# Re-timing the row gathers of a PEER layer: slot transfers, early loads, weight rows and a gate pass moved

## The chip, the cores and the metric

The kernel runs on one core of one Trainium2 chip. The metric is the device time of one execution in microseconds (us); lower is better. The time before is 1664.05 us, the median of three executions (1662.84 to 1665.58).

## What is computed

One decoder layer over 256 tokens of width 2048: two kinds of attention, a layer norm, the PEER block, a second norm, a gated embedding and a third norm. The change touches the PEER block alone. In the reference it is, cut short:

```
q = (xt @ wq).reshape(t, 8, 256)                 # 8 heads, two halves a and b
sa, sb = q_a @ keys[0].T, q_b @ keys[1].T        # 128 scores for each half
va, ia = top_k(sa, 16);  vb, ib = top_k(sb, 16)
top, sel = top_k(va[..., :, None] + vb[..., None, :], 16)
eidx = (ia * 128 + ib)[sel];  gates = softmax(top)
act = gelu(u[eidx] . x);  out = sum(gates * act * v[eidx])
```

So each token picks 16 of 16384 experts in each of 8 heads, and needs the 2048 numbers of each picked expert's row in two tables, `u` and `v` (128 MB each).

## The kernel before, in words

**Two ways through the experts.** For the first 88 tokens (`NSP`) the rows are gathered token by token. One such *sparse gather* (L1042) brings 128 rows, 1 MB, into one of four buffers `gb`, and VectorE multiplies it: 88 gathers of `u` rows (L1008, dot products), then 88 of `v` rows (L1018, weighted sums `y`). That makes 176. For the other 168 tokens (`NDT`) the kernel works densely by blocks of 128 experts. A first part of the experts (`SEG1`, 56 blocks) takes `u` whole: `u_block` multiplies a block of `u` with the tokens and keeps the activations in `A0`, `A1`. For the remaining 72 blocks' worth, only experts that some token picked are listed: 48 *listed* blocks (`NBLK[1]`), gathered into `uf` (L1400), transposed and multiplied. The `v` side has 39 *gathered* blocks for the first part (`NBLK[0]`) and 48 listed ones, each a 1 MB gather into `vf` or `vx` (L1400) and sixteen 128x128 matrix multiplications (L1489, each shown as two records) with 128 or 168 token columns, as `cols` says.

**The order of the stages** is: query and scores head half by head half (16 steps `hh`); dense `u` (56 blocks); listed `u` (48 blocks); `v` of the 39 gathered blocks; `v` of the 48 listed ones; the residuals and the second norm; the gated embedding.

**Weights of the gathered blocks.** After dense `u`, a first gate pass (`all_gates`, `gate_work`) multiplies the gates into `A0`, `A1`; these go to the scratch `s_w` in HBM by eight transfers on SyncE's queue, and each gathered block fetches its 128 weight rows back with a gather of its own into `wc`. A second gate pass does the same for the listed blocks' weights, `WL`. It has 57 groups of up to three tokens (14 for the 40 tokens of the first half, 43 for the 128 of the second), and nearly every group takes two steps of the generator, 118 in all. `half`, called twice in each gathered block, runs them. For each group VectorE makes one-hot tables (L715, L1098), ScalarE scales (L1096), TensorE multiplies into `ps_G` (L1107, L1108), VectorE multiplies into `WL` (L1116).

**What sets the order.** Generators are advanced at fixed places by `run`. The sparse gathers are paced by `gathers(n)`, which adds `n` to a running sum and starts one gather for each whole unit; the constants `GQ`, `GU`, `GUF`, `GUT`, `GUL`, `GV` are gathers per step or block of each stage. The result of gather k is used when gather k+3 is started. A scheduler with a time estimate of its own then fixes each engine's instruction order at build time; from there on every engine takes its instructions in that order. All row gathers (sparse, `uf`, `vf`, `vx`, `wc`) and the small *slot transfers* `eig` (L825), which lay out the picked expert numbers for the sparse gathers, are issued by GpSimd (POOL).

**The top-k of the first 128 tokens** is done by `topk_work` in batches of heads (`BATCH`): first head and count. A batch's top-k on VectorE is followed by `head_slots`, which computes the expert numbers (L821) and issues the slot transfer (L825). Then the generator does the other 128 tokens' top-k (`second`), and beside it `first_flags`, which first transposes the picked indices of the first 128 tokens on TensorE (`index_T`, L856).

**Early loads.** Five blocks of `u` are loaded ahead into `early`, one at each of the steps hh = 2 to 6; the dense `u` stage uses them first.

Of the kernel before, what the change touches and what calls it, by code (L numbers as in the profile page):

```python
# [9 lines left out]
F32 = mybir.dt.float32  # L10
# [9 lines left out]
P = 128  # L20
# [26 lines left out]
NBLK = tuple(map(sum, CAPS))  # L47
# [10 lines left out]
NDT = T - NSP  # L58
# [1 line left out]
SELB = 8  # L60
CAND = ((0, 3, 16), (3, 16, 4))
NCAND = sum((i1 - i0) * w for i0, i1, w in CAND)
BATCH = ((0, 1), (1, 2), (3, 2), (5, 2), (7, 1))
NGB = 4


GQ = 1.7
GU, GUF, GUT = 0.80, 0.92, 0.50
GUL, GV = (1.10, 1.50), (0.62, 0.88)
GSCALE = 2.0 ** 15  # L70
GB = 3

EARLY, HEARLY = 5, 2
OHB = 4

STAG, LEAD, NVX = 3, 4, 4
FBC = 12
NZERO = 3
WF = 5
# [90 lines left out]
def build(tc, a, out):  # L170
    nc = tc.nc
    pools = Pools(tc)
# [20 lines left out]
    at = pools.open("at", "left", bufs=2)  # L193
# [95 lines left out]
    def load(dst, src):  # L289
        tc.keep_in_program_order(nc.sync.dma_start(dst, src))  # L290
# [262 lines left out]
    def ln_rows(pool, which):  # L553
        gr = pool.tile([P, D], F32, name="g_row", tag="g_row")
        br = pool.tile([P, D], F32, name="b_row", tag="b_row")
        load(gr, a["ln_g"][which:which + 1, :].to_broadcast([P, D]))
        load(br, a["ln_b"][which:which + 1, :].to_broadcast([P, D]))
        return gr, br
# [53 lines left out]
    def affine(xt, c, gr, br):  # L612
        s = slice(c * 512, (c + 1) * 512)
        nc.gpsimd.tensor_tensor(xt[:, s], xt[:, s], gr[:, s], op=ALU.mult)
        nc.gpsimd.tensor_tensor(xt[:, s], xt[:, s], br[:, s], op=ALU.add)
# [3 lines left out]
    def spill_x1():  # L619
        gr, br = ln_rows(rowp, 0)  # L620
        yield 4
        for c in range(NCH):
            affine(x1[0], c, gr, br)
            yield 4
        load(a["s_x1"], x1[0])
        spilled.append(0)
# [78 lines left out]
    keep = tc.keep_in_program_order  # L705
# [112 lines left out]
    def head_slots(h):  # L818

        c = slice(h * TOPK, (h + 1) * TOPK)  # L820
        nc.vector.scalar_tensor_tensor(eg[:NSPR, 0, h], iaN[:NSPR, 0, c], float(NKEY),  # L821
                                       ibN[:NSPR, 0, c], op0=ALU.mult, op1=ALU.add)
        t0, n = GROUPS[0]
        m = n // PH
        nc.gpsimd.dma_start(  # L825
            eig[0][:, 0, h * m:(h + 1) * m],
            eg[t0:t0 + n, 0, h].rearrange("t (r c) -> t r c", c=m))

    def topk_work():
        nc.vector.tensor_copy(io128, io128f)  # L830
        for h0, n in BATCH:
            for _ in topk_heads(0, h0, n):
                pass
            for h in range(h0, h0 + n):
                head_slots(h)
            yield
        for i in range(1, len(GROUPS)):
            slots(i, 0, by_slot(i, 0))

        second, first, flags = topk_heads(1, 0, PH), gates(0), first_flags()  # L840
        for step, _ in enumerate(second):
            if step > 2:
                next(first, None)
            next(flags, None)
            yield
        for _ in first:
            pass
        yield from index_T(1)
        yield from second_flags(gates(1), flags)
# [117 lines left out]
    def gathers(n):  # L967

        nonlocal due
        due += n  # L970
        while due >= 1:
            due -= 1
            run(sparse, 1)
# [243 lines left out]
    idxV, idxW, over = {}, {}, []  # L1217
# [117 lines left out]
    def run(work, n):  # L1335

        for _ in range(n):
            if next(work, "end") == "end":
                return True
        return False  # L1340
# [9 lines left out]

    steps = 1
    work = topk_work()
    sparse = sparse_work()
    bg.add(spill_x1(), 4)
    for hh in range(2 * PH):
        if hh == HEARLY:

            assert spilled
            pools.close("rowp", "x1p")
            lsp = pools.open("lsp", "right", bufs=1)  # L1360
            iaT, ibT = (lsp.tile([P, T, 2], F16, name=nm) for nm in ("iaT", "ibT"))
            iaF, ghf = (lsp.tile([P, T], F32, name=nm) for nm in ("iaF", "ghf"))
            gl2 = lsp.tile([P, T, 2], F16, name="gl2")
            a0p = pools.open("a0p", "right", bufs=1)
            A0 = a0p.tile([P, SEG0, NDT], F32, name="A0")
            earlyp = pools.open("earlyp", "right", bufs=1)
            early = [earlyp.tile([P, D], F32, name=f"early{ia}") for ia in range(EARLY)]
        if HEARLY <= hh < HEARLY + EARLY:
            load(early[hh - HEARLY], a["peer_u"][hh - HEARLY])
        query(hh)  # L1370
        if hh in [2 * (h0 + n) for h0, n in BATCH]:
            run(work, 1)
        if hh > 2:
            gathers(GQ)
    bg.flush()
    run(work, 1)
    for ia in range(SEG1):
        if ia == EARLY:
            pools.close("earlyp")
            a1p = pools.open("a1p", "right", bufs=1)  # L1380
# [12 lines left out]
    marked = False  # L1393
    order = [(i, b) for i in range(2) for b in range(NBLK[i])]

    def cols(i, b):
        return (N0, P) if b < CAPS[i][0] else (0, NDT)

    def rows_of(dst, src, idx, b):
        keep(nc.gpsimd.indirect_dma_start(  # L1400
            out=dst, out_offset=None, in_=src,
            in_offset=bass.IndirectOffsetOnAxis(ap=idx[:, b:b + 1], axis=0),
            bounds_check=src.shape[0] - 1, oob_is_err=False))
        return dst

    def WL_of(b):
        c0 = min(b, CAPS[1][0]) * P + max(b - CAPS[1][0], 0) * NDT
        return WL[:, c0:c0 + cols(1, b)[1]]

    def slot(name):  # L1410
        return sup.tile([P, D], F32, name=name, tag="wf", bufs=WF)

    fetched = []
    taken = 0

    def fetch():
        nonlocal taken
        i, b = order.pop(0)
        k = taken % (WF + NVX)
        taken += 1  # L1420
        if k % 2 and k < 2 * NVX and not i and b < NBLK[0] - WF:
            vf = vxp.tile([P, D], F32, name="vx", tag="vx", bufs=NVX)
        else:
            vf = slot("vf")
        if i:
            w = WL_of(b)
        else:
            c0, n = cols(i, b)
            w = wcp.tile([P, NDT], F32, name="wc", tag="wc", bufs=WF + NVX + 1)
            rows_of(w, a["s_w"].rearrange("p a t -> (p a) t"), idxW[i], b)  # L1430
            w = w[:, c0:c0 + n]
        rows_of(vf, a["v_rows"], idxV[i], b)
        fetched.append((i, b, vf, w))

    def rows_T(uf, c, pool, tpool):

# [14 lines left out]
    stored = False  # L1451
    work = all_gates(ohp, A0, A1, WL)
# [13 lines left out]
    for k in range(2):  # L1466
        turn(k)
    for b in range(NBLK[1]):
        if b == NBLK[1] - LEAD:
            assert stored  # L1470
            pools.close("a1p", "a0p")
            vxp = pools.open("vxp", "right", bufs=1)
            wcp = pools.open("wcp", "right", bufs=1)
        ps = pbank(pp, "ps_u")
        c0, n = cols(1, b)
        for c in range(4):
            turn(4 * b + c + 2)
            rows_mm(ps, turned.pop(0), c, c0, n)
            if b >= 2 and (c or n > P) and not stored:
                run(work, 1)  # L1480
        keep(nc.scalar.activation(WL_of(b), ps[:, :n], AF.Gelu_apprx_tanh))
        if b >= NBLK[1] - LEAD:
            fetch()
        gathers(GUL[n > P])
    pools.close("utp")
    def v_mm(d, i, b, vf, w, last):
        c0, n = cols(i, b)
        o = psv[d // 3][:, d % 3 * NDT + c0:d % 3 * NDT + c0 + n]
        return nc.tensor.matmul(o, vf[:, d * P:(d + 1) * P], w, start=False,  # L1489
                                stop=last and (d % 3 == 2 or d == ND - 1))  # L1490
# [16 lines left out]
    def v_blocks(n, ahead, between=lambda d: None):  # L1507

        for _ in range(n):
            while order and len(fetched) <= (ahead if order[0] < (0, NBLK[0] - WF) else LEAD):  # L1510
                fetch()
            block = fetched.pop(0)
            for d in range(ND):
                v_mm(d, *block, False)
                if d % 8 == 7:
                    between(d)
            gathers(GV[cols(*block[:2])[1] > P])

    psv = [v_bank(pp, 3 * NDT) for _ in range(4)] + [v_bank(pa, n * NDT) for n in (3, 1)]
    done = False  # L1520

    def half(d):
        nonlocal done
        if not done:
            done = run(work, 2)

    for b in range(NBLK[0]):
        if b == NBLK[0] - LEAD:
            more = nc.values_load(total[0:1, 0:1], min_val=0, max_val=NIA * NKEY)
        v_blocks(1, LEAD + NVX, half)  # L1530
    assert done
    for dst, src in zip(("s_ia", "s_ib", "s_gl"), (iaT, ibT, gl2)):
# [99 lines left out]
    with tc.If(more > 0, preferred_fallthrough_block=True, label="rest"):  # L1632
# [5 lines left out]
        for ia in range(NIA):  # L1638
            i = int(ia >= SEG1)
            vf, uf, _ = spare  # L1640
            nc.gpsimd.dma_start(vf, a["v_rows"][ia * NKEY:(ia + 1) * NKEY, :])
            wc = fbp.tile([P, NDT], F32, name="wc_", tag="wc_")
# [395 lines left out]
```

## Time and profile before

| | us |
|---|---|
| median of three executions | 1664.05 |
| the profiled execution | 1664.92 |
| its span, first to last instruction | 1663.1 |
| TensorE busy in it | 1610.7 |
| VectorE / ScalarE / GpSimd busy | 1056.0 / 735.7 / 603.1 |
| data moved | 518.53 MB, mean 312 GB/s |

The stages in the span: query from about 414 to 534, dense `u` to 824, listed `u` to 1132, `v` of the gathered blocks to 1300.9, the end of the second gate pass alone to 1318.6, `v` of the listed blocks to 1554. In the profile PE is TensorE, DVE VectorE, ACT ScalarE, POOL GpSimd, SP SyncE. A row of a timeline gives the start, the duration, the engine and line, and in brackets the idle time before it with what ended it; a row of waits gives who waited for whom, then total us, number and longest. The rows themselves stand in the prediction.

### The profile page before, as it was taken

The numbers are of one execution on the slowest core, as the hardware profiler recorded it, in microseconds if no ns is written. First come the engines' busy times: TensorE is split into PE (matmuls) and PEld (weight loads), VectorE is DVE, ScalarE is ACT, GpSimd is POOL, SyncE is SP. The second block draws the span as 40 slices with busy tenths as digits, with TensorE's granted clock in tenths as the row PEclk, the third lists the DMA queues.
The fourth block names the chain that finished last, engine by engine and source line by source line (L and its number), as shares of the span: only waits on it lengthen the run. The fifth ranks groups of instructions, "written<-read, shape, count | busy, mean of one in ns | idle before, by whom it ended". The sixth has DMA issues, their size and how long they took to land. (4 is left out here: it accounts for less than half of the span.)

```text
span 1663.1 us, 30575 instructions
## 1 busy us (share of the span) xinstructions
PE 1610.7 (97%) x11666; PEld 1491.9 (90%) x11666; DVE 1056.0 (63%) x2557; ACT 735.7 (44%) x1740; POOL 603.1 (36%) x538
## 2 busy tenths in 40 slices
PE   9999999999999899999999999999999698899998
PEld 7888888877889899999999999998999688899787
DVE  5555488865377899676667888723455844450776
ACT  5687458753111276956566666530222200000552
POOL 0133023201244425121544434556886755521000
PEclk9999999999999999999999999999999799999999
DMA  8654654475798699999999999999999999996571
GB/s 297 199 164 153 239 166 140 161 301 184 297 377 343 266 422 409 390 359 374 354 421 388 369 346 346 364 344 411 412 380 367 357 421 420 421 386 205 200 269 51
DMA packets 90606, 518.53 MB, mean 312 GB/s; under 512 B 12300, under 2 KB 15436, under 8 KB 38314
## 3 DMA queue, kind: packets, MB, share of 16 engines
q0 software_dynamic: 47984, 330.83, 50.5%
q1 hardware_dynamic: 40742, 182.55, 30.0%
q10 hardware_dynamic: 1728, 3.15, 0.5%
q8 instruction: 92, 1.51, 0.4%
q14 instruction: 60, 0.49, 0.1%
HBM read 508.47 MB, written 10.18 MB: 312 GB/s over the span
## 5 line engine op out<-in xcount | busy, mean ns | idle before, releaser
L131 DVE TENSOR_TENSOR wl<-wf,wh 128x1024 fp32r<-128x1024 f32 (+1 forms) x199 | 212.7, 1091 | 139.3 <-ACT wh L130 137.6
L130 ACT CAST wh<-wf 128x1024 fp32r<-128x1024 f32 (+1 forms) x199 | 172.0, 892 | 258.6 <-DMA wf<-ple_gate 145.9
L1018 DVE SCALAR_TENSOR_TENSOR y<-gb,ew,y 128x2048 f32<-128x2048 f32 x78 | 183.2, 2349 | 145.7 <-DMA gb<-v_rows,eig 144.5
L221 PE MATMUL ps_u<-XF,wf 128*128 128x168 f32 x1632 | 251.3, 311 | 0.0
L221 PEld LDWEIGHTS ps_u<-XF,wf 128*128 128x128 f32 x1632 | 235.5, 191 | 3.0
L1489 PE MATMUL ps_v<-WL,vf 128*128 128x128 f32 (+1 forms) x1536 | 204.9, 297 | 18.0 <-DMA vf<-v_rows,idxV 15.5
L1448 PE MATMUL ps_u<-XF,uT 128*128 128x128 f32 (+1 forms) x1536 | 220.2, 288 | 0.0
L1489 PEld LDWEIGHTS ps_v<-WL,vf 128*128 128x128 f32 x1536 | 201.4, 200 | 20.4 <-DMA vf<-v_rows,idxV 17.2
L1008 DVE SCALAR_TENSOR_TENSOR gb<-gb,xq 128x2048 f32<-128x2048 f32 x88 | 200.5, 2285 | 22.6 <-DMA gb<-u_rows,eig 21.4
L1448 PEld LDWEIGHTS ps_u<-XF,uT 128*128 128x128 f32 x1536 | 199.1, 191 | 0.7
L209 PE MATMUL ps_qk<-X,wh 128*128 128x512 f32 x512 | 185.2, 401 | 0.0
L1042 POOL DMA_INDIRECT gb<-u_rows,eig x88 | 105.3, 1196 | 210.0 <-DVE eqb L715 42.7
L1442 ACT COPY uT<-ps_T 128x512 f32<-128x512 f32 x192 | 111.7, 587 | 115.4 <-PE ps_T L1439 115.0
L1042 POOL DMA_INDIRECT gb<-v_rows,eig x88 | 131.5, 1494 | 53.4 <-issue 20.4
L1096 ACT ACTIVATE hi<-eq,ghf 128x56 f16<-128x56 f16 (+2 forms) x336 | 87.0, 325 | 141.4 <-DVE eq L715 137.8
L211 PE MATMUL ps_qk<-X,wl 128*128 128x256 f32 x512 | 145.7, 285 | 0.0
L1400 POOL DMA_INDIRECT vf<-v_rows,idxV x72 | 92.0, 1278 | 113.0 <-PE ps_v L1489 85.8
L209 PEld LDWEIGHTS ps_qk<-X,wh 128*128 128x128 f32 x512 | 96.4, 188 | 21.9 <-issue 1.0
L1439 PE MATMUL ps_T<-ident,uf 128*128 128x128 f32 x768 | 113.1, 274 | 2.4 <-DMA uf<-u_rows,idxV 2.4
L221 PE MATMUL ps_q<-XF,wf 128*128 128x256 f32 x512 | 114.6, 381 | 0.2 <-ACT eb L590 0.2
L221 PEld LDWEIGHTS ps_q<-XF,wf 128*128 128x128 f32 x512 | 96.1, 191 | 13.2 <-ACT eb L590 0.9
L1400 POOL DMA_INDIRECT uf<-u_rows,idxV x48 | 60.3, 1257 | 123.2 <-PE ps_T L1439 112.6
(366 smaller groups left out, 2909.6 us busy)
## 6 DMA issues: line engine op xcount, KB each, us to landing
wf<-peer_u SPq DMA_DIRECT2D x51, 1024.0 KB
wf<-w_qk SPq DMA_DIRECT2D x64, 512.0 KB
wf<-w_out SPq DMA_DIRECT2D x32, 512.0 KB
wf<-peer_wq SPq DMA_DIRECT2D x16, 1024.0 KB
wf<-ple_gate SPq DMA_DIRECT2D x16, 1024.0 KB
wf<-w_v SPq DMA_DIRECT2D x16, 512.0 KB
wf<-w_sv SPq DMA_DIRECT2D x15, 512.0 KB
early<-peer_u SPq DMA_DIRECT2D x5, 1024.0 KB
```

Source lines behind the costliest of these rows:

```text
L130: self.order(nc.scalar.copy(wh, src))
L131: self.order(nc.vector.tensor_tensor(wl, src, wh.bitcast(F32), op=ALU.subtract))
L209: nc.tensor.matmul(ps, wh[:, j * P:(j + 1) * P], xt[:, dt, :], start=dt == 0, stop=False)
L211: nc.tensor.matmul(ps[:, :T], wl[:, j * P:(j + 1) * P], xt[:, dt, :T], start=False, stop=dt == ND - 1)
L221: nc.tensor.matmul(ps[:, :T - t0], wf[:, dt * P:(dt + 1) * P], xt[:, dt, t0:], start=dt == 0, stop=dt == ND - 1)
L1008: keep(nc.vector.scalar_tensor_tensor(g, g, 1.0, xq[i], op0=ALU.mult, op1=ALU.mult, accum_out=eact[i][:, j:j + 1]))
L1018: keep(nc.vector.scalar_tensor_tensor(ys[i], g, ew[i][:, j:j + 1], ys[i], op0=ALU.mult, op1=ALU.add))
L1042: keep(nc.gpsimd.indirect_dma_start(out=g, out_offset=None, in_=a[kind], in_offset=bass.IndirectOffsetOnAxis(ap=eig[i][:, 0, j:j + 1], axi ...
L1400: keep(nc.gpsimd.indirect_dma_start(out=dst, out_offset=None, in_=src, in_offset=bass.IndirectOffsetOnAxis(ap=idx[:, b:b + 1], axis=0), bo ...
L1439: nc.tensor.transpose(ps[:, j * P:(j + 1) * P], uf[:, (4 * c + j) * P:(4 * c + j + 1) * P], ident)
L1448: nc.tensor.matmul(ps[:, :n], uT[:, j * P:(j + 1) * P], XF[:, d, NSP + c0:NSP + c0 + n], start=d == 0, stop=d == ND - 1)
L1489: return nc.tensor.matmul(o, vf[:, d * P:(d + 1) * P], w, start=False, stop=last and (d % 3 == 2 or d == ND - 1))
```

## The change

Five edits, made together:

1. `BATCH` becomes (0,1), (1,1), (2,2), (4,2), (6,2), and a `yield` stands between a batch's top-k and its slot transfers, so the transfers are issued one step hh later than the top-k (`starts`). The last batch has two heads instead of one, and its slot transfers come in the first dense `u` block. `first_flags` starts at step 6 of `second` instead of step 0.
2. The five early loads are issued at hh = 6, 8, 10, 12, 14.
3. In the last four listed `u` blocks only the four row transfers `vf` are issued, all into slots that `uf` leaves; the pools of `vx` and `wc` are opened after the last listed `u` block, and the weight rows `wc` follow then, ordered behind the last of these transfers (`issue_after(behind.ins)`). The order of slots and extra buffers changes with it: five slots, then four `vx`.
4. `half` runs 4 steps a block only in the first eight gathered blocks and 3 after that, instead of 4 throughout.
5. The rates: `GQ` 1.7 to 2.0; 2.2 gathers a block (`GUE`) in the last six listed `u` blocks, instead of 1.5; `GV` from 0.62 and 0.88 (narrow and wide blocks) to 0.42 and 0.80 for the gathered and 0.42 and 0.85 for the listed blocks.

```
-BATCH = ((0, 1), (1, 2), (3, 2), (5, 2), (7, 1))
+BATCH = ((0, 1), (1, 1), (2, 2), (4, 2), (6, 2))
-GQ = 1.7
+GQ = 2.0
-GUL, GV = (1.10, 1.50), (0.62, 0.88)
+GUL, GUE = (1.10, 1.50), 2.20
+GV = (0.42, 0.80), (0.42, 0.85)
-EARLY, HEARLY = 5, 2
+HEARLY, WHEN = 2, (6, 8, 10, 12, 14)
+EARLY = len(WHEN)
...
             for _ in topk_heads(0, h0, n):
                 pass
+            yield
             for h in range(h0, h0 + n):
                 head_slots(h)
             yield
...
-            next(flags, None)
+            if step > 5:
+                next(flags, None)
...
-        if HEARLY <= hh < HEARLY + EARLY:
-            load(early[hh - HEARLY], a["peer_u"][hh - HEARLY])
+        if hh in WHEN:
+            k = WHEN.index(hh)
+            load(early[k], a["peer_u"][k])
         query(hh)
-        if hh in [2 * (h0 + n) for h0, n in BATCH]:
+        if hh in starts or hh - 1 in starts:
             run(work, 1)
...
-        if k % 2 and k < 2 * NVX and not i and b < NBLK[0] - WF:
+        if k >= WF and not i and b < NBLK[0] - WF:
             vf = vxp.tile([P, D], F32, name="vx", tag="vx", bufs=NVX)
...
+    def weights():
+        for block in fetched:
+            i, b, _, w = block
+            if w is None:
+                c0, n = cols(i, b)
+                w = wcp.tile([P, NDT], F32, name="wc", tag="wc", bufs=WF + NVX + 1)
+                rows_of(w, a["s_w"].rearrange("p a t -> (p a) t"), idxW[i], b)
+                block[3] = w[:, c0:c0 + n]
...
-        gathers(GUL[n > P])
+        gathers(GUL[n > P] if b < NBLK[1] - LEAD - 2 else GUE)
     pools.close("utp")
+    assert stored
+    pools.close("a1p", "a0p")
+    vxp = pools.open("vxp", "right", bufs=1)
+    wcp = pools.open("wcp", "right", bufs=1)
+    with tc.issue_after(behind.ins):
+        weights()
+        for _ in range(NVX + 1):
+            fetch()
+            weights()
...
-            gathers(GV[cols(*block[:2])[1] > P])
+            gathers(GV[block[0]][cols(*block[:2])[1] > P])
...
-            done = run(work, 2)
+            done = run(work, 1 + (d < 8 or at < 8))
```

More of the change, by code (lines that the diff above doesn't have):

```diff
@@ L1354, in build @@
     bg.add(spill_x1(), 4)
+    starts = [2 * (h0 + n) for h0, n in BATCH]
     for hh in range(2 * PH):
@@ L1394, in build @@
     order = [(i, b) for i in range(2) for b in range(NBLK[i])]
+    behind = None
     def cols(i, b):
@@ L1399, in rows_of @@
     def rows_of(dst, src, idx, b):
-        keep(nc.gpsimd.indirect_dma_start(
+        nonlocal behind
+        behind = keep(nc.gpsimd.indirect_dma_start(
             out=dst, out_offset=None, in_=src,
@@ L1424, in fetch @@
             vf = slot("vf")
[L1425 to L1431, printed above, removed]
-        rows_of(vf, a["v_rows"], idxV[i], b)
-        fetched.append((i, b, vf, w))
+        rows_of(vf, a["v_rows"], idxV[i], b)
+        fetched.append([i, b, vf, WL_of(b) if i else None])
+    def weights():
[6 more added lines that the diff above has]
+                block[3] = w[:, c0:c0 + n]
     def rows_T(uf, c, pool, tpool):
@@ L1468, in build @@
     for b in range(NBLK[1]):
[L1469 to L1473, printed above, removed]
         ps = pbank(pp, "ps_u")
@@ L1511, in v_blocks @@
                 fetch()
+                weights()
             block = fetched.pop(0)
@@ L1516, in v_blocks @@
                     between(d)
-            gathers(GV[cols(*block[:2])[1] > P])
+            gathers(GV[block[0]][cols(*block[:2])[1] > P])
     psv = [v_bank(pp, 3 * NDT) for _ in range(4)] + [v_bank(pa, n * NDT) for n in (3, 1)]
     done = False
+    at = 0
     def half(d):
@@ L1529, in build @@
             more = nc.values_load(total[0:1, 0:1], min_val=0, max_val=NIA * NKEY)
+        at = b
         v_blocks(1, LEAD + NVX, half)
```

## The prediction

> **What bounds the kernel now.** I read the page first, then TensorE's waits, then windows cut at the stages of the PEER block, then the timelines of POOL, DVE and PE around the start of v.
>
> ```profile
> PE 1610.7 (97%) x11666; PEld 1491.9 (90%) x11666; DVE 1056.0 (63%) x2557; ACT 735.7 (44%) x1740; POOL 603.1 (36%) x538
> ...
> PEclk9999999999999999999999999999999799999999
> DMA  8654654475798699999999999999999999996571
> ```
>
> PE is busy 97% of the span, so at most about 52 us of idle time can go, and what the clock loses with it. The clock digit falls once, in the 32nd of 40 slices (1289 to 1330), and the DMA digits are at 9 from the 15th to the 36th: the second half of the kernel runs with the transfer engines nearly full.
>
> ```profile
> PE ps_v L1489 <- DMA vf<-v_rows,idxV: 15.5, 6, 5.0
> PE ps_G L1107 <- DVE eq L715: 8.7, 5, 2.8
> PE ps_gT L856 <- DVE ibN L775: 3.3, 1, 3.3
> PE ps_G L1107 <- DVE WL L1116: 3.1, 3, 2.1
> PE ps_T L1439 <- DMA uf<-u_rows,idxV: 2.4, 1, 2.4
> PE ps_x1T L598 <- ACT XF L547: 2.4, 1, 2.4
> PE ps_v L1489 <- DVE WL L1116: 2.3, 1, 2.3
> PE ps_gT L856 <- DVE iaN L775: 2.1, 1, 2.1
> ```
>
> All but the x1T row lie where the change works: rows of v that are late (15.5), the second gate pass (8.7 + 3.1 + 2.3 = 14.1), the index transposes (5.4) and one listed u row (2.4).
>
> ```profile
> 534.00:582.00 48.00, 42.57 (x288) 41.62 (x287) 42.16 (x154) 12.91 (x39) 18.45 (x23) 0.96 0.74 287
> 566.00:570.00 4.00, 4.00 (x22) 3.91 (x21) 3.72 (x22) 2.84 (x9) 2.78 (x6) 0.74 1.03 421
> 1039.00:1132.00 93.00, 90.59 (x768) 89.42 (x767) 44.23 (x112) 40.08 (x89) 51.74 (x41) 1.00 0.93 357
> 1132.00:1300.90 168.90, 168.87 (x1548) 165.47 (x1546) 89.54 (x248) 36.30 (x146) 119.57 (x89) 1.00 0.99 391
> 1300.90:1318.60 17.70, 3.32 (x53) 2.44 (x52) 17.70 (x51) 6.04 (x23) 12.69 (x7) 0.63 0.94 351
> 1318.60:1455.00 136.40, 120.77 (x987) 119.20 (x988) 61.35 (x28) 4.43 (x8) 77.70 (x57) 0.92 1.01 416
> 1455.00:1515.00 60.00, 60.00 (x419) 59.52 (x418) 21.86 (x22) 0.00 (x0) 15.87 (x15) 1.00 0.87 339
> ```
>
> Columns: length, busy us of PE, PEld, DVE, ACT, POOL, then granted clock, DMA share, GB/s. In the gathered blocks of v (to 1300.9) PE never waits. Then it stands 14.4 of 17.7 us while VectorE, busy all 17.7, finishes the gate pass. In the listed blocks (to 1455) it loses 15.6 us at a clock of 0.92 with the DMA at its ceiling of 1.01. After 1455 PE is full again, as the sparse gathers run out.
>
> **The start of v.** Why the pass ends late is seen 130 us earlier.
>
> ```profile
> 1088.36 2.31 POOL L1400 DMA_INDIRECT uf<-u_rows,idxV  x1 [4.60 <-PE ps_T L1439]
> 1101.33 1.00 POOL L1400 DMA_INDIRECT wc<-s_w,idxW  x1 [10.66 <-issue]
> ...
> 1119.56 0.99 POOL L1400 DMA_INDIRECT uf<-u_rows,idxV  x1 [0.31 <-issue]
> 1120.86 0.96 POOL L1042 DMA_INDIRECT gb<-v_rows,eig  x1 [0.30 <-issue]
> ```
>
> ```profile
> 1129.39 2.35 DVE L1018 SCALAR_TENSOR_TENSOR y<-gb,ew,y 128x2048 f32<-128x2048 f32 x1 [28.09 <-DMA gb<-v_rows,eig]
> ...
> 1176.88 2.35 DVE L1018 SCALAR_TENSOR_TENSOR y<-gb,ew,y 128x2048 f32<-128x2048 f32 x1 [8.32 <-DMA gb<-v_rows,eig]
> 1179.15 0.18 DVE L715 TENSOR_TENSOR eq<-io,blkT 128x54 f16<-128x54 f16 x1
> ```
>
> ```profile
> 1147.59 3.74 PE L1489 MATMUL ps_v<-wc,vx 128*128 128x128 f32 x32
> 1151.16 3.74 PE L1489 MATMUL ps_v<-wc,vf 128*128 128x128 f32 x32
> ...
> 1186.89 0.17 PE L1107 MATMUL ps_G<-hi,ohb 128*128 128x18 f16 x1
> ```
>
> From 1088 to 1101 POOL stands before the first weight row, which reads what the stores to s_w write:
>
> ```profile
> 1063.58 5.03 SPq L290 DMA_DIRECT2D s_w<-A  x8
> ```
>
> Then POOL issues weight rows and extra rows, and only at 1120 the last listed u row and the next sparse gather. VectorE, in program order, waits 28 us for that gather and for more behind it, so the pass's first table comes at 1179 and its first product at 1186.9, 55 us into v. Started that late, it ends late.
>
> **Part by part: slots, flags and early loads.**
>
> ```profile
> POOL eig L825 <- DVE eg L821: 49.9, 4, 21.8
> ```
>
> In the query POOL waited 49.9 us on slot transfers whose numbers were not computed, with the sparse gathers queued behind. Issued one step later, most of that goes; PE is full there, so this buys only earlier gathers: 13 steps x 2.0 = 26 against 13 x 1.7 = 22. The early loads move from a slice with DMA digit 7 (the 11th) to two with 9 and 8; wf has five slots of lead, which hides that, and if it doesn't, a query load that is late costs PE up to a load, 2.5 us. The flags start six steps later, at 1.5 steps a block four blocks of dense u (56 blocks in the 290 us from 534 to 824, so 21 us), so PE reaches the index transposes after VectorE; the last batch now has two heads, which takes some of this back (VectorE is busy 42.2 of 48 us). Gap 5.4 plus clock 48 x 0.04 = 1.9 makes 7.3. Bounds -7.3 to +3.3 (one such wait more than now); I take -6, nearer the full gain, since 21 us of delay is far more than the 5.4 to be covered.
>
> The clock: after two waits of 2.1 and 3.3 us it was 0.74 from 566 to 570, and 0.63 in the 17.7 us of the pass, whose longest gap is 2.8. The Trainium skill (TensorE: Matmul & The Clock Gate, HAM oscillation) says that only idle gaps above about 3.4 us throttle the clock. By it the 1.9 us would not be there to win, and the gain would be up to 1.9 smaller. The trace speaks against that limit here; the rows' clocks are used.
>
> **Weight rows behind listed u.** The 2.4 us wait for the last listed u row goes with the weight rows ahead of it: -2.4 (bounds -2.4 to 0). New is that v's first block waits for its own weight row, now issued behind the last of four row transfers, and behind it queue four more weight rows, five v blocks and the gathers.
>
> ```profile
> wc<-s_w,idxW POOLq DMA_INDIRECT x29, 8.6
> ```
>
> That is us from issue to landing in gathered v, with the DMA at 0.99. If POOL issues one landing ahead of PE's need it costs 0; if POOL issues it only as PE arrives, 8.6, and twice that if a second landing lies ahead of it (2.2 gathers in each of six blocks fill the queue). I take 4, in the middle of the first two, since the last of the four row transfers gets its slot about a block before PE is done with listed u.
>
> **Gathers and the gate pass, by two limits.** A 1 MB transfer takes 1.05 MB / 416 GB/s = 2.5 us at the ceiling. Started by the program, from the rates: before 22 in the query, 67 by the end of dense u (45 in both kernels), 127 by the end of listed u (30 x 1.10 + 18 x 1.50 = 60), 155 after gathered v (24 x 0.62 + 15 x 0.88 = 28), 174 at listed block 30 (30 x 0.62). After: 26, 71, 135 (30 x 1.10 + 12 x 1.50 + 6 x 2.20 = 64), 157 (24 x 0.42 + 15 x 0.80 = 22), 171 with the fractions carried (30 x 0.42).
>
> ```profile
> L1042 POOL DMA_INDIRECT gb<-u_rows,eig x88: 933/967/3086, 454.0 to 937.4; - x88
> L1042 POOL DMA_INDIRECT gb<-v_rows,eig x31: 933/940/2932, 943.6 to 1127.2; - x31
> ```
>
> Up to 1132, POOL had issued 88 + 31 = 119: 8 behind the program. So 55 gathers stood between there and block 30. After the change, the last six blocks ask for 4.2 more while the row 1039 to 1132 has 0.08 x 93 = 7.4 us unused, three gathers; I take 124 issued, so 47 remain: 8 fewer, 20 us of DMA. The unused shares of the next two rows (0.02 x 168.9 + 0.07 x 17.7) add 4.6; the later gathers beside the wide blocks take back about 1. DMA limit: -23.
>
> PE's limit over the same stretch: idle 14.4 + 15.6, clock 0.08 x 136.4 = 10.9, together -41, less the 4 at v's start: -37. The DMA limit is smaller and is what I take. It presumes that the pass doesn't hold PE. Its steps need 8 x 4 + 86 / 3 blocks = 36.7 of the 39 instead of 118 / 4 = 29.5; the cover is VectorE's time, which must no longer stand behind late gathers.
>
> Sum: -6 - 2.4 - 23 = -31. The profiled execution took 1664.92 (span 1663.1, 1.8 around it), 0.9 above the median. 1664.9 - 31.4 - 0.9 = 1632.6, so 1633. Bounds of the terms: DMA term -37 (PE's limit) to -10 (below).
>
> **Rivals.** *The moved gathers don't get through earlier* (chance 0.24). Listed u already has a share of 0.93 and 8 gathers of arrears; if its extra 4.2 only lengthen the arrears, just the four from the query are gained, 10 us: -6 - 2.4 - 10 gives 1646, within 1641 to 1658. For it: the last six listed u blocks ask for 13 gathers and four v transfers, 17 x 2.5 = 43 us, and PE is through them in about 38 (48 blocks from 824 to 1132). Against: POOL stood 10.7 us and then held the gathers for twenty more.
>
> *Slower: the thinner gate pass holds the listed blocks* (0.13). Its place is the change from gathered to listed v. If its first product comes 55 us into v as now, 7.2 more blocks end it later. A narrow block is 3.57 us by the two starts above, a wide one, as the last of the gathered ones are, 4.45 by these:
>
> ```profile
> 1458.36 4.72 PE L1489 MATMUL ps_v<-WL,vf 128*128 128x168 f32 x32
> 1462.81 0.51 PE L1064 MATMUL ps_yn<-wh,sel 128*64 128x512 f32 x1
> ```
>
> That is 32 us, and the wait becomes 14 + 32 = 46. The DMA catches up in it, so 15.6 + 10.9 go; -6 - 2.4 - 26.5 + 32 + 4, and 7 us for the clock, which a wait like that brings down (0.63 above), gives +8, 1672. With these terms it turns slower from a first product about 47 us into v. Against: the 28 us hole that caused the lateness is taken away.
>
> *No difference* (0.07). The order in which POOL issued weight rows ahead of a listed u row shows that the scheduler's own estimate decides; it may lay the gathers out as late as now: 1664.
>
> **How the numbers follow.** Forecast 0.56, with its own range 1616 to 1640. Range 1616 to 1659: it leaves out the slower case and no difference, 0.20. A measurement here tells about 0.2% (3.3 us) from no change; faster by more 0.80, within 0.07, slower 0.13.
>
> **What would show it.** Right: no wait of ps_T for uf and none over 1 us of ps_gT; the first ps_G of the second pass within 30 us of v's start; the hole at its end under 8 us; PE's wait for vf in listed v under 6 us with a DMA share still near 1; about 124 gathers issued by v's start. The first row would be a new wait of ps_v for wc of some 4 us. Wrong: a hole of 20 us or more before listed v, or a wait of over 10 us for wc, or a vf wait as long as now.

## The result, and the profile after

The changed kernel takes 1658.21 us (median of 13 runs, 1651.44 to 1661.56) where the kernel before takes 1665.58 on the same chip (13 runs, 1662.84 to 1668.35): a ratio of 0.9947, 95% interval 0.9933 to 0.9961. By the ratio it is faster by about 9 us (7.4 by the medians), not by the 31 that were forecast. The profiled execution took 1654.64 (span 1652.8; before 1663.1), 3.6 us below its median.

From the page of the changed kernel, the rows that answer to those of before:

```profile
PE 1603.2 (97%) x11666; PEld 1486.8 (90%) x11666; DVE 1058.0 (64%) x2557; ACT 732.4 (44%) x1740; POOL 585.0 (35%) x542
...
PEclk9999999999999999999989999999999879999999
DMA  8554654485799799999999999999999899996661
```

There are now two dips of the clock: the 21st slice (826 to 868) is new, and the one near the 33rd (1322 to 1364) is the old one, a slice later. TensorE's waits (who waited for whom, total us, number, longest) tell what stands in them:

```profile
PE ps_G L1111 <- DVE eq L717: 8.7, 4, 2.8
PE ps_G L1111 <- DVE lo L1102: 7.4, 1, 7.4
PE ps_G L1111 <- DVE WL L1120: 7.2, 7, 2.7
PE ps_v L1505 <- DVE WL L1120: 4.5, 1, 4.5
...
PE ps_v L1505 <- DMA vf<-v_rows,idxV: 2.7, 1, 2.7
PE ps_G L1111 <- ACT hi L1100: 2.6, 1, 2.6
```

The index transposes (5.4 us before) and the listed u row (2.4) are gone, and late rows of v fell from 15.5 to 2.7 (one wait, in the gathered blocks). But the gate passes rose: the first has a wait of 7.4 that it did not have, and the rows of the second add up to 23.0 (8.7 + 7.2 + 4.5 + 2.6), where they were 14.1.

Windows cut at the borders of the stages, first before, then after (length, busy us of PE, PEld, DVE, ACT and POOL, then granted clock, DMA share, GB/s):

```profile
534.43:825.02 290.59, 283.78 (x2130) 276.80 (x2128) 228.25 (x651) 174.09 (x535) 91.75 (x117) 0.99 0.93 368
825.02:1134.88 309.86, 307.45 (x3140) 303.38 (x3139) 206.20 (x702) 177.39 (x467) 149.64 (x118) 1.00 0.95 370
1318.64:1480.00 161.36, 145.76 (x1157) 143.72 (x1158) 78.29 (x46) 4.43 (x8) 86.65 (x65) 0.94 1.01 417
```

```profile
533.84:817.42 283.58, 281.41 (x2120) 275.27 (x2119) 218.37 (x603) 167.16 (x526) 92.89 (x117) 1.00 0.95 375
817.42:1136.61 319.19, 311.60 (x3158) 307.00 (x3155) 227.63 (x721) 180.83 (x476) 148.04 (x115) 0.98 0.95 368
1136.61:1305.00 168.39, 165.23 (x1514) 163.96 (x1513) 82.17 (x233) 34.42 (x139) 119.91 (x94) 0.99 0.98 390
1305.00:1332.63 27.63, 5.02 (x79) 3.64 (x75) 27.56 (x67) 7.61 (x29) 12.12 (x10) 0.56 0.94 355
1332.63:1490.00 157.37, 157.37 (x1290) 156.81 (x1291) 59.79 (x40) 4.43 (x8) 79.17 (x61) 0.98 0.99 399
```

Dense u is 7.0 us shorter and listed u 9.3 longer. The hole before listed v, 14.4 us of idle TensorE before, is now 27.63 - 5.02 = 22.6 at a clock of 0.56. The listed blocks run through without a wait. By the borders (v ends at 1554.4 before and 1543.8 after):

| stretch | before | after | forecast | measured |
|---|---|---|---|---|
| dense and listed u | 600.4 | 602.8 | -8.4 | +2.3 |
| v, gathered and listed | 419.5 | 407.2 | -23 | -12.3 |
| all else | 643.1 | 642.8 | 0 | -0.3 |

The sums of the two columns are -31.4 and -10.3, so half of the miss lies in u and half in v.

**Where the u part went.** VectorE's timeline at the start of listed u, before and after: the last row number of the list (`idxV`), the sparse dot products, the first one-hot table of the first gate pass.

```profile
810.95 0.20 DVE L1332 SCALAR_TENSOR_TENSOR idxV<-ps_list,ib 128x40 uint32<-128x40 f32 x1
811.06 2.28 DVE L1008 SCALAR_TENSOR_TENSOR gb<-gb,xq 128x2048 f32<-128x2048 f32 x1
...
829.50 2.29 DVE L1008 SCALAR_TENSOR_TENSOR gb<-gb,xq 128x2048 f32<-128x2048 f32 x1 [5.93 <-DMA gb<-u_rows,eig]
831.71 0.24 DVE L715 TENSOR_TENSOR eq<-io,iaT 128x168 f16<-128x168 f16 x1
```

```profile
824.26 0.20 DVE L1336 SCALAR_TENSOR_TENSOR idxV<-ps_list,ib 128x40 uint32<-128x40 f32 x1
824.38 2.28 DVE L1012 SCALAR_TENSOR_TENSOR gb<-gb,xq 128x2048 f32<-128x2048 f32 x1
...
836.30 2.29 DVE L1012 SCALAR_TENSOR_TENSOR gb<-gb,xq 128x2048 f32<-128x2048 f32 x1 [3.00 <-DMA gb<-u_rows,eig]
838.79 2.29 DVE L1012 SCALAR_TENSOR_TENSOR gb<-gb,xq 128x2048 f32<-128x2048 f32 x1 [0.19 <-DMA gb<-u_rows,eig]
841.01 0.24 DVE L717 TENSOR_TENSOR eq<-io,iaT 128x168 f16<-128x168 f16 x1
```

Six dot products stand between list and table in both. The list is ready 13.3 us later, so the table is 9.3 us later, while TensorE, 7 us ahead of its old course, comes to the first product at 834.3 and waits until 841.7.

**Where the v part went.** The changed kernel's POOL and VectorE around the start of v at 1136.6:

```profile
1118.94 0.95 POOL L1046 DMA_INDIRECT gb<-v_rows,eig  x1 [0.30 <-issue]
1122.78 0.99 POOL L1409 DMA_INDIRECT vf<-v_rows,idxV  x1 [2.88 <-PE ps_T L1450]
1124.08 1.01 POOL L1409 DMA_INDIRECT wc<-s_w,idxW  x1 [0.31 <-issue]
...
1144.28 0.96 POOL L1046 DMA_INDIRECT gb<-v_rows,eig  x1 [0.30 <-issue]
```

```profile
1151.04 2.35 DVE L1022 SCALAR_TENSOR_TENSOR y<-gb,ew,y 128x2048 f32<-128x2048 f32 x1 [18.37 <-DMA gb<-v_rows,eig]
...
1189.19 2.35 DVE L1022 SCALAR_TENSOR_TENSOR y<-gb,ew,y 128x2048 f32<-128x2048 f32 x1 [2.93 <-DMA gb<-v_rows,eig]
1191.46 0.18 DVE L717 TENSOR_TENSOR eq<-io,blkT 128x54 f16<-128x54 f16 x1
```

POOL's stand of 10.7 us is gone, but its run of weight and extra rows, now behind listed u, still keeps the sparse gathers away from 1119 to 1144. VectorE still waits 18 us, and then does eight results `y`, from 1151 on, before the pass's first table at 1191.5, 54.9 us into v (44.3 before, by the same borders). In the kernel before eight results end there too, the first of them begun 0.6 us ahead of v. What moved is the moment at which the gathers go on: 14.0 us ahead of v before (1120.9 against 1134.9), 7.7 us into v now. At the other end of the pass, `y` results and groups take turns on VectorE, each `y` a wait of TensorE (VectorE first, then TensorE):

```profile
1312.42 2.35 DVE L1022 SCALAR_TENSOR_TENSOR y<-gb,ew,y 128x2048 f32<-128x2048 f32 x1
1314.68 0.24 DVE L717 TENSOR_TENSOR eq<-io,blkT 128x144 f16<-128x144 f16 x1
```

```profile
1315.78 0.20 PE L1111 MATMUL ps_G<-hi,ohb 128*128 128x48 f16 x1 [2.72 <-DVE eq L717]
```

### The profile page after: what moved, and what is told of

It reads as the page before. It is cut to its first block, busy times and chain, and to the rows that moved or that the text cites. A ratio compares the mean times of both kernels' runs of the same rounds, so it can differ in the third digit from the quotient of the medians.

```text
span 1652.8 us, 30585 instructions
## 1 busy us (share of the span) xinstructions
PE 1603.2 (97%) x11666; PEld 1486.8 (90%) x11666; DVE 1058.0 (64%) x2557; ACT 732.4 (44%) x1740; POOL 585.0 (35%) x542
## 5 line engine op out<-in xcount | busy, mean ns | idle before, releaser
L1505 PE MATMUL ps_v<-WL,vf 128*128 128x128 f32 (+1 forms) x1536 | 197.1, 291 | 4.7 <-DVE WL L1120 4.5
L1505 PEld LDWEIGHTS ps_v<-WL,vf 128*128 128x128 f32 x1536 | 195.3, 196 | 5.6 <-DVE WL L1120 4.7
L1046 POOL DMA_INDIRECT gb<-v_rows,eig x88 | 121.5, 1381 | 66.2 <-DVE eq L717 24.0
L1505 PE MATMUL ps_v<-wc,vf 128*128 128x128 f32 (+1 forms) x800 | 106.4, 292 | 2.7 <-DMA vf<-v_rows,idxV 2.7
```

Of the source, the lines that this page charges most:

```text
L1046: keep(nc.gpsimd.indirect_dma_start(out=g, out_offset=None, in_=a[kind], in_offset=bass.IndirectOffsetOnAxis(ap=eig[i][:, 0, j:j + 1], axi ...
```

## The experiments

Two theories. A, *late start*: gathers that the program starts in listed u but POOL issues only in v put their results on VectorE ahead of the pass's first table, so the pass starts, and ends, late. Below, the gathers started but not yet issued are called *arrears*. B, *thin pass*: 3 steps a block are too few. For u: C, the later flags moved a wait from the transposes to the first gate pass.

Each ratio is to the kernel before on the same chip and in the same group of runs. This is needed: in one group (f) the kernel before takes 1665.7 us, in the others 1688 to 1691. Differences are taken within a group; a ratio of one group set beside that of another is an indication only, since the changed kernel itself has 0.9945 in f and 0.9918 in h. f0 and h0 are plain copies of the changed kernel, i2 is one of the kernel before; all others but e3 and e4 are the changed kernel with the edit shown. *Hole* is TensorE's waits, from the start of v to the first listed block, for VectorE or ScalarE at the products of the second gate pass and at that block (14.4 in the kernel before, 23.0 in the changed kernel). *Late rows* is its waits for `vf` in listed v, *first table* the us from the first product of v. Hole, late rows and first table are from one trace of each kernel.

| group | kernel | us | ratio (95%) | first table | hole | late rows |
|---|---|---|---|---|---|---|
| e | e1_pass4 | 1667.7 | 0.9886 (0.9868-0.9904) | 55 | 6.8 | 7.7 |
| e | e2_gue12 | 1664.3 | 0.9855 (0.9837-0.9872) | 23 | 2.8 | 0 |
| e | e3_slots | 1682.7 | 0.9968 (0.9955-0.9981) | 27 | 9.1 | 14.8 |
| e | e4_weights | 1676.6 | 0.9932 (0.9917-0.9948) | 42 | 13 | 14.4 |
| f | f0_after | 1658.0 | 0.9945 (0.9927-0.9964) | 54 | 23.0 | 0 |
| f | f1_flags0 | 1657.3 | 0.9955 (0.9939-0.9971) | 70 | 23.8 | 0 |
| f | f2_dots | 1650.1 | 0.9904 (0.9888-0.9920) | 70 | 27.1 | 0 |
| f | f3_early | 1642.8 | 0.9859 (0.9839-0.9880) | 23 | 9.4 | 0.9 |
| g | g1_both | 1670.1 | 0.9878 (0.9861-0.9895) | 25 | 19.1 | 0 |
| g | g2_both_pass4 | 1666.4 | 0.9857 (0.9836-0.9878) | 25 | 2.4 | 9.1 |
| g | g3_pass4 | 1667.0 | 0.9862 (0.9844-0.9879) | 55 | 7.8 | 8.6 |
| g | g4_edits123 | 1680.0 | 0.9940 (0.9924-0.9956) | 28 | 8.9 | 13.8 |
| h | h0_after | 1674.9 | 0.9918 (0.9905-0.9932) | 54 | 23.3 | 0 |
| h | h1_pass4 | 1667.4 | 0.9864 (0.9849-0.9879) | 56 | 9.3 | 8.6 |
| h | h2_early | 1662.1 | 0.9837 (0.9824-0.9851) | 23 | 10.8 | 1.4 |
| h | h3_both_pass4 | 1666.2 | 0.9855 (0.9840-0.9870) | 25 | 3.8 | 12.4 |
| i | i1_early_pass4 | 1658.5 | 0.9816 (0.9794-0.9837) | 22 | 1.0 | 5.7 |
| i | i2_before | 1689.9 | one run | 37 | 15.2 | 17.5 |

**The thin pass undone** (e1, g3 and h1 are the same kernel).

```
-            done = run(work, 1 + (d < 8 or at < 8))
+            done = run(work, 2)
```

> The changed kernel with one edit undone: the second gate pass again at 4 steps a gathered block throughout. Theory A (the pass ends late because it starts late: VectorE has to finish the results of the sparse gathers that stand ahead of the first table in its order, and these gathers are 11 behind the program): the first product of the pass stays at about 62 us after the start of v, the stretch of TensorE waits before listed v keeps at least 15 of its 22.5 us, and the time is within 5 us of the changed kernel. Rival B (the thinner pass itself makes the hole): the first product also stays, but the waits before listed v fall below 8 us and the time falls by 12 to 20 us.

> The changed kernel with the second pass at 4 steps a block throughout, once more, to have it on the same chip as others. On the other chip it was 0.9886 of the kernel before where the changed kernel is 0.9945 here. If that holds on this chip, it is 8 to 12 us below the changed kernel's, and the waits before listed v are under 8 us; if the difference was the chip's, its ratio is 0.993 to 0.996.

> The changed kernel with the second gate pass at 4 steps a block throughout. If the thin pass makes the waits before listed v: waits there under 8 us and 6 to 14 us faster than the changed kernel beside it. If its late start makes them, and the transfers' total what follows: within 4 us of the changed kernel.

Beside the changed kernel it is 7.6 us faster (h1, 1667.4 against 1674.9). The first table stays where it was and the hole falls from 23.3 to 9.3, so B holds: with the same late start, the rate decides the hole. A part comes back, as TensorE reaches the listed blocks sooner than their rows. TensorE's waits in h1:

```profile
PE ps_v L1505 <- issue: 11.1, 18, 1.2
PE ps_G L1111 <- DVE lo L1102: 9.7, 1, 9.7
PE ps_v L1505 <- DMA vf<-v_rows,idxV: 8.6, 4, 2.6
PE ps_G L1111 <- DVE WL L1120: 7.0, 4, 2.5
PE ps_v L1505 <- DVE WL L1120: 2.3, 1, 2.3
```

**Fewer gathers ahead of the pass.**

```
-GUL, GUE = (1.10, 1.50), 2.20
+GUL, GUE = (1.10, 1.50), 1.20
```

> The changed kernel with one number changed: 1.2 instead of 2.2 gathers a block in the last six listed u blocks, so 6 fewer gathers started by the program before v. Theory A: 6 fewer results stand ahead of the pass's first table, so its first product comes 20 to 30 us earlier (32 to 42 us into v), the waits before listed v fall from 22.5 us to below 12, and listed v may wait again for late rows by up to 6 x 2.5 = 15 us: time between 12 us faster and 3 us slower than the changed kernel. Rival B (only the rate of the pass counts): hole as before within 4 us, and the later gathers make it 5 to 15 us slower. Rival C (the six gathers were never issued before v anyway): the count of gathers issued by the start of v stays at 124 within 2.

Six gathers fewer are started in listed u, and yet 124 are issued by the start of v, as in the changed kernel: those six had only lengthened the arrears. Two results instead of eight are still to be done in v ahead of the first table, which comes at 23 us; the hole is 2.8, although the pass still runs at 3 steps. Beside e1, which up to v is the changed kernel, the table comes 32 us earlier. So the gathers put ahead of the pass matter too, as A has it; whether by the time of the first table is taken up below. The price is at the end: the last sparse rows are late, and TensorE waits 9.7 us for VectorE behind listed v.

**Some of the six given to gathered v** (f3 and h2 are the same kernel).

```
-GUL, GUE = (1.10, 1.50), 2.20
-GV = (0.42, 0.80), (0.42, 0.85)
+GUL, GUE = (1.10, 1.50), 1.20
+GV = (0.55, 0.85), (0.42, 0.85)
```

> The changed kernel with 1.2 instead of 2.2 gathers a block in the last six listed u blocks, and about four of these six given to the gathered blocks of v (0.55 and 0.85 a block instead of 0.42 and 0.80). Theory A: the first product of the second gate pass comes within 40 us of the start of v, the waits before listed v stay under 6 us although the pass runs at 3 steps a block from the ninth block on, the wait of about 10 us after listed v for the last sparse rows falls below 4 us, and the time is 4 to 12 us below the changed kernel's. Rival (the transfers' total sets the end): the waits only change places, and the time is within 3 us of the changed kernel's.

> The changed kernel with 1.2 instead of 2.2 gathers a block in the last six listed u blocks and 0.55 and 0.85 instead of 0.42 and 0.80 in the gathered v blocks. On a chip with the kernel before at about 1666 us it was 15 us below the changed kernel, a ratio of 0.9859. If that is a matter of this kernel and not of the chip, it is 10 to 18 us below the changed kernel here, first product of the second pass under 40 us into v.

It is 15.2 us below the changed kernel in group f, more than the 4 to 12 expected, and 12.9 in h. In f3's windows of gathered v, the hole, and the first 30 listed blocks, TensorE idles 11.27 - 2.11 = 9.2 us in the hole, not under 6 as expected, and hardly any late rows follow (0.9):

```profile
1134.81:1306.50 171.69, 167.97 (x1552) 166.74 (x1550) 89.53 (x267) 39.12 (x157) 124.46 (x95) 0.98 0.98 389
1306.50:1317.77 11.27, 2.11 (x34) 1.61 (x35) 10.97 (x30) 2.91 (x11) 9.82 (x5) 0.60 0.90 302
1317.77:1430.33 112.56, 111.65 (x978) 111.41 (x979) 41.37 (x22) 4.43 (x8) 60.59 (x48) 0.98 1.01 420
```

From the start of v to the end of listed block 30 it takes 1430.3 - 1134.8 = 295.5 us. The kernel before takes 1453.7 - 1134.9 = 318.8, the changed one 1444.8 - 1136.6 = 308.2.

**The flags' delay undone.**

```
-            if step > 5:
-                next(flags, None)
+            next(flags, None)
```

> The changed kernel with the delay of the flags undone: they start at step 0 of the second half's top-k again, all else as changed. Theory A (the delay only moves a wait: the list of the gathered blocks is ready 13 us later, and the first gate pass's first table stands behind it and six sparse dot products on VectorE): the waits of the index transposes come back with 2 to 6 us, the wait of 7 to 10 us at the first product of the first gate pass goes, and the time is within 4 us of the changed kernel. Rival (the delay is a gain as forecast): the transposes' waits come back, the first gate pass waits as now, and it is 4 to 8 us slower.

No difference (1657.3 against 1658.0, the intervals overlap): C holds in its sum, but not in its parts. The transposes do not wait here either. VectorE's timeline shows why (f1, then the kernel before):

```profile
551.61 0.22 DVE L777 TENSOR_TENSOR ibN<-eqsel 128x32 f32<-128x32 f16 x1
```

```profile
564.95 0.19 DVE L775 TENSOR_TENSOR ibN<-eqsel 128x16 f32<-128x16 f16 x1
```

The last indices are ready 13 us earlier, and the last batch of the first 128 tokens now has two heads (32 columns instead of 16). So undoing the delay doesn't bring the wait back, and by this timeline it was the new batches that took it away, though no run has them alone; the delay only moved the list. Without it dense u takes 291.0 us instead of 283.7, listed u 315.0 instead of 320.2, and the wait at the first product is 4.1 instead of 9.5.

**Fewer dot products ahead of the first gate pass.**

```
-GU, GUF, GUT = 0.80, 0.92, 0.50
+GU, GUF, GUT = 0.80, 0.92, 0.20
```

> The changed kernel with 0.2 instead of 0.5 sparse gathers a block in the last ten dense u blocks: three gathers fewer started there, so four instead of six dot products stand ahead of the first gate pass's first table on VectorE. Theory A: the wait at the first product falls by 2 x 2.3 = 4.6 us and by up to 3.0 us more (the dots' own wait for rows), to under 3 us; the three gathers are lost from the early part, worth up to 7 us at the transfers' ceiling later: time from 7 us faster to 2 us slower. Rival (the wait is for the list, not for the dots): the wait stays within 1.5 us of what it is.

Four dot products instead of six stand ahead of the first table, and the wait is gone. Dense and listed u of f2, with TensorE busy for all of listed u:

```profile
532.92:818.58 285.66, 282.88 (x2125) 277.05 (x2123) 216.38 (x602) 167.95 (x529) 88.69 (x114) 0.99 0.94 373
818.58:1127.75 309.17, 309.17 (x3153) 304.53 (x3149) 219.82 (x718) 179.13 (x473) 145.69 (x110) 1.00 0.94 366
```

Together 594.8 us instead of 603.9 in the copy beside it; of these 9 us, v (hole 27.1) takes back 5. The time is 7.9 us below the copy's, a little more than the 7 expected at most.

**Single parts on the kernel before.** e3 is edits 1 and 2 with `GQ` at 2.0; e4 is edit 3; g4 is edits 1, 2, 3 and `GQ`, with edit 4 and the rest of edit 5 undone.

```
 e3:  -GQ = 1.7
      +GQ = 2.0     and the hunks of edits 1 and 2
 e4:  the hunks of fetch, weights, rows_of and issue_after alone
 g4:  +GUL, GUE = (1.10, 1.50), 1.50
      +GV = (0.62, 0.88), (0.62, 0.88)
      +            done = run(work, 2)
```

> The kernel before with edits 1 and 2 alone (batches, slot transfers a step later, flags from step 6, early loads at heads 6 to 14) and 2.0 gathers a step in the query. By the prediction's term of -6 and four gathers more before dense u: 6 to 12 us faster than the kernel before. If the new wait of 7.4 us at the first product of the first gate pass (six sparse dot products ahead of the first table on VectorE) belongs to these edits, that wait is here too, and the gain is 0 to 4 us.

> The kernel before with edit 3 alone: weight rows behind listed u, everything else as before. By the prediction's term: the wait of 2.4 us for the last listed u row goes and a wait for weight rows of 0 to 8.6 us comes, so between 2.4 us faster and 6 us slower. Theory A says beside it that the first product of the second pass moves by no more than 10 us, since the same 15 issues of POOL still stand between the last gathers of listed u and the next ones, and the waits before listed v stay within 5 us of 14.4. The other reading, that POOL's stand of 10.7 us made the pass late, has it 10 to 30 us earlier, with the time 5 to 14 us faster.

> Edits 1, 2 and 3 with the higher rate of the query, but with the gate pass at 4 steps and the other rates of gathers as before (1.5 a block to the end of listed u, 0.62 and 0.88 in v). If the thin pass and the gathers put ahead of it are what ate the forecast gain, this kernel, without them, is faster than the changed one: ratio 0.985 to 0.990, waits before listed v under 10 us, waits for late rows in listed v of 5 to 16 us. If the moved gathers are where the gain comes from, it is slower than the changed kernel: ratio 0.995 to 1.000.

e3 has the new wait at the first gate pass (8.8 us), so it belongs to edits 1 and 2; its gain of 5.7 us (3.2 to 7.6 by the interval) lies across the two bands expected. e4 is 11.8 us faster, outside what was forecast for it, and not by the pass: its hole is 13 and its first table 42, no earlier than in the kernel before in a group as slow (i2: 15.2 and 37). What it lacks is a wait in listed u that i2 has there (last section): listed u takes 309.9 us in e4 and 325.8 in i2. That compares two groups, so it is an indication. g4 disagrees with its first expectation: without the moved gathers and without the thin pass its ratio (0.9940) is no lower than the changed kernel's in group h (0.9918), with 13.8 us of late rows. It lies just below the band of the second. Within the group, g3 and g4 differ only in the rates of listed u and of v, and g3, which has those of edit 5, is 13.0 us faster. So edit 5 is where a gain of the changed kernel in v comes from, and edit 4 spends a part of it (7.6 us by h1 against h0).

**The repairs together.** g1 has the hunks of f2 and f3; g2 and h3 have those and 4 steps; i1 has those of f3 and 4 steps.

> The changed kernel with both repairs together: 0.2 instead of 0.5 gathers a block in the last ten dense u blocks, and 1.2 instead of 2.2 in the last six listed u blocks with 0.55 and 0.85 instead of 0.42 and 0.80 in the gathered v blocks. If the two waits are separate losses, the gains of the two kernels that had one repair each add up: 7.9 + 15.2 = 23 us below the changed kernel, a ratio to the kernel before of 0.981 or a little more. If the transfers' total sets the end, the second repair buys nothing: ratio 0.985 to 0.987, with late rows in listed v or after it in place of the wait that goes.

> As the kernel with both repairs, and the second gate pass at 4 steps a block throughout. The waits before listed v (10 us with the second repair alone, which still has 3 steps a block) should fall below 4 us; TensorE then reaches the listed rows sooner, and of the 6 to 8 us a part, by the changed kernel with 4 steps alone (7.7 us of waits for rows), comes back as waits for late rows: between 6 us faster and 2 us slower than both repairs.

> All three repairs: fewer gathers at the end of dense u, fewer at the end of listed u and some of them in gathered v, and the pass at 4 steps a block throughout. If the waits that each removes are separate losses: 20 to 28 us below the changed kernel. If late rows take their place: 10 to 16 us below, with waits for late rows of 8 us or more in listed v and of over 4 us for the last sparse rows behind it.

> The changed kernel with the gathers moved (1.2 a block at the end of listed u, 0.55 and 0.85 in gathered v) and the second gate pass at 4 steps a block throughout. With the gathers moved alone, 10 us of waits are left before listed v at 3 steps. If 4 steps take those without a price: 4 to 9 us below that kernel, ratio 0.978 to 0.982 of the kernel before. If late rows take their place, as with all three repairs: ratio 0.983 to 0.988, waits for late rows in listed v of 6 us or more.

The losses do not add up. g1 has 0.9878, higher than either of its expectations, with a hole of 19. In h3 the hole is 4 us, but late rows take 12.4 and the last sparse rows hold TensorE another 4.4; it is 8.7 us below the changed kernel, less than h2 with one repair (12.9). The three gathers that f2 saves in dense u are missing later. Without that saving, i1 has 1.0 us of hole and 5.7 of late rows, at 0.9816 the lowest ratio of all, 30.7 us below the kernel before; but its interval overlaps that of h2, so that it beats h2 is not shown.

**What the hole goes with.** The time of the first table does not set the hole. f1's table comes 16 us later than f0's, with a hole 0.8 us longer; g1's comes 25 us into v and h2's 23, and their holes are 19.1 and 10.8 (all four at 3 steps). What the hole does go with is the number of sparse results that VectorE does from the start of v to the end of the pass:

| steps a block | results, and hole in us |
|---|---|
| 3 after the eighth block | 22: 2.8 (e2); 24: 9.4, 10.8 (f3, h2); 26: 19.1 (g1); 28: 23.0, 23.3 (f0, h0); 29: 23.8, 27.1 (f1, f2) |
| 4 throughout | 19: 1.0 (i1); 20: 2.4, 3.8 (g2, h3); 22: 6.8, 7.8, 9.3 (e1, g3, h1); 23: 8.9 (g4); 24: 9.1, 13.0, 15.2 (e3, e4, i2); 27: 14.4 (before) |

So the form in which theory A was put, late start and therefore late end, is too narrow. By these counts it is how many results VectorE still has to do among the steps of the pass, together with the steps a block. This is read from the traces and not shown by a run of its own: a longer hole also leaves room for more results.

## Why the prediction was wrong

**The step that failed.** "It presumes that the pass doesn't hold PE. ... the cover is VectorE's time, which must no longer stand behind late gathers." The failed step is that presumption. VectorE stands behind late gathers as before: eight results end within v ahead of the first table, as many as in the kernel before. The program has started 135 gathers by the start of v and POOL has issued the 124 that were counted, so the arrears are 11, where the prediction had 8 for the kernel before, and VectorE works off the results in program order. At 3 steps a block the pass then ends 196 us into v (184 before), and TensorE idles 22.6 us. By the prediction's own signs, the first product was to come within 30 us of v's start and came at 58, and a hole of 20 us or more was to tell that it is wrong. The rival "the thinner gate pass holds the listed blocks" had the mechanism, with the hole at 22.6 instead of its 46, too little to turn the change slower; its condition, a first product 55 us into v, came about (58). "The 28 us hole that caused the lateness is taken away" was the argument against it, and 18 us of it were still there: behind listed u, the weight rows hold the gathers just as they did in it, and this stand of VectorE now lies mostly within v.

**The first rival** ("the moved gathers don't get through earlier") was right about the extra gathers of listed u: 124 are issued by the start of v at 2.2 a block (the changed kernel, e1, g3), at 1.5 (g4) and at 1.2 (e2). The higher rate only lengthened the arrears, so the prediction's count of 124 came true, but not for the reason given. What brought it up from 120 is not shown. The measured 1658.2 lies at the upper end of the range (1616 to 1659) and of this rival's band (1641 to 1658). That it lies in the range is luck: the rival's sum has no hole of 23 us in it, nor a wait in u.

**The DMA term of -23** is about right where the pass is nearly out of the way. Between the start of v and the end of listed block 30 POOL issues 53 gathers in the kernel before, 46 in the changed one (forecast 55 and 47) and 44 in f3. f3 takes 23.3 us less for this stretch (318.8 to 295.5). The changed kernel takes 10.7 less, since the hole, up by 8.2 us and at a clock of 0.56, lies in the same stretch. The choice of the DMA limit over TensorE's fits as well: in h1, i1 and h3 late rows return as the hole shrinks.

**Slots, flags and early loads, -6.** Dense u gained 7.0. What failed is where it was left: nobody was named as next, and next was the first gate pass (7.4, and 0.98 for the clock of listed u). The cause was wrong as well: the transposes' wait stays away without the 21 us of delay (f1), so the rest of these edits ended it, by the timelines the batches, and no gain from the delay can be measured. Of the four gathers that the higher rate of the query should start early, one was issued more (68 against 67 by the start of listed u).

**The listed u row, -2.4**, went as said. **The wait for weight rows, 4 us**, did not come; a wait of 2.7 for a row of v stands in its place.

**The clock.** The Trainium skill (TensorE: Matmul & The Clock Gate, HAM oscillation) gives idle gaps above about 3.4 us as what throttles. The trace after speaks against that limit as the one before did: of the waits from 1305 to 1332.6 all but the last (4.5) are under 2.9 us, and the clock is 0.56; from 1305 to 1328, ahead of that last wait, it is 0.57.

## What to carry to other kernels

Where results come through an engine that works in order, count what the program has started and not what the queue has issued: work that is started earlier but not finished earlier only stands in front of the next pass. When a wait goes, name who waits next, by the time at which each input of the next stage is ready, before the gain is booked. And where transfers bound a stretch, moving them pays only while nothing else holds the engine; repair the order first, since two repairs that draw on the same transfers do not add.

## What the runs showed of the hardware

The kernel before takes 1665.6 and 1665.7 us in two groups of runs and 1688 to 1691 in the four others, 1.4% more. The record doesn't tie this to a chip: it gives the same chip number, 8, to group f (1665.7) and to group i (1689.2). The difference is not spread evenly. In i2's trace dense u takes 290.8 us, as in the first trace (290.6), but listed u 325.8 instead of 309.9 and gathered v with the hole 193.5 instead of 183.8. There TensorE and ScalarE stand although nothing that the profile shows is late: ScalarE's copies `uT`, with up to 10.75 us of idle time ahead of one, hold TensorE, and the trace doesn't name what released them. From i2's waits:

```profile
PE ps_u L1448 <- ACT uT L1442: 14.0, 4, 8.2
...
PE ps_v L1489 <- issue: 5.8, 8, 1.1
```

And ten us at the start of v in h0, the changed kernel in a group as slow, where the transfer engines are full (share 0.99) and TensorE's gaps, which wait for nothing that the profile shows (`issue`), are each of 1.7 us at most:

```profile
1148.00:1158.00 10.00, 5.44 (x21) 4.60 (x20) 2.59 (x2) 0.00 (x0) 6.90 (x6) 0.64 0.99 378
```

In h0 and i2 such gaps of TensorE lie where the DMA share, over some 10 us around them, is 0.88 to 1.02. But the changed kernel's first trace has a share of 0.98 in gathered v without them, so full transfer engines alone don't make them. What the engines wait for there stays open, since no run changed it. Here too the clock falls, to 0.64.
